# Down waves and gate steps in turn, gate weights half a chunk at a time, and a 26th buffer, in a mixture-of-experts layer

## The chip, the cores and the metric

The kernel runs on one core of a Trainium2 chip. The metric is the device time of one execution in microseconds (us). The core has a matrix engine (TensorE, shown as PE, its weight loads as PEld), a vector engine (VectorE, DVE), a scalar engine (ScalarE, ACT), a general engine (GpSimd, POOL) and a sequencer for transfers (SyncE, SP). 16 DMA engines move data between device memory (HBM) and the on-chip buffer (SBUF). Matmuls write to PSUM.

## The reference

One layer of a decoder on 256 tokens of width 2048, all in float32:

```
proj = rms_norm(x) @ w_in                       # 2048 x 4608: conv gates, q, k, v
h = x + [norm(conv(...)), norm(attention(...))] @ w_out     # 2048 x 2048
xt = rms_norm(h)
# top group of 4, then the top 2 of its 8 experts, for each token
h = h + sum over 2 experts of w * (silu(xt @ w_gate[e]) * (xt @ w_up[e])) @ w_down[e]
out = h + sigmoid(rms_norm(h) @ w_ple_gate) * (p @ w_ple)   # w_ple_gate 2048 x 2048
```

There are 32 experts, each with gate and up weights of 2048 x 512 and down weights of 512 x 2048, so every weight of every expert is read once: 403 MB of the 479 MB that the kernel reads.

## The kernel before, in words

**Buffers and transfers.** Nearly all data lives in a ring of `NSLOT` = 25 buffers of 8 KB per partition (1 MiB each). `want` (L63) lists every weight load in order. `pump` (L66) issues loads from that list, on SP's queue, as long as a buffer is free after what `reserve` holds back; `free` (L80) returns buffers and calls `pump`. So the order of the list and the places of the `free` calls in the program fix when each load can start. SP works in order: a load whose buffer is still being read holds up all later ones.

**Projections.** The input projection and the output projection (L332 to L823) split each float32 weight tile into a rounded part (`nc.scalar.copy`, L340) and a remainder (`tensor_sub`, L341), and multiply with three matmuls. The tiles of this stage leave the ring as it ends, and loads for the experts move in.

**Experts.** `select` and `gather` (L919, L938) pick up to 32 tokens for each of four experts, a *wave*, and transpose them into `xg`: eight waves. `gate_up` (L955) runs a wave's gate and up products; its rows are taken four at a time (`j4`), gate first, then up, and after each such group the four experts' buffers are freed. For the first row group of wave 0 the weights come in tiles that hold one row block of all four experts. There the gathers of wave 0 stand between the products:

```
                    if first and jj == 1:
                        gather(0, 4 if n == 0 else 12)
                if first and n == 0:
                    gather(0, 8)
```

After a wave's hidden values are transposed, `down_rows` (L1003) multiplies them with the down weights: waves 0 to 3 for all 2048 columns, waves 4 to 7 for the first 1024. `outputs` (L1051) scales a result into a rounded part `yh` (ScalarE) and a remainder `yl` (VectorE), and `scatter` (L1058) adds it to the tokens by matmul.

**The tail.** The output has four column chunks of 512 (`TC`, L149). Once a chunk of h is complete, `rows` (L1125) transposes it into `hs`, and eight *gate steps* (`gate_step`, L1149, twelve matmuls each) multiply it with 512 rows of `w_ple_gate`; `prep_pg` (L1114) splits those weights two steps ahead into three buffers. Chunks 0 and 1 are complete after `down_rows(7)`. For chunks 2 and 3 waves 4 to 7 run as `down_wave` (L1092), four loads each. Lines 1225 to 1247 set the order by hand: all eight gate steps of chunk 0, then chunk 2's four waves with chunk 1's steps, then chunk 3's four waves with chunk 2's steps. Then chunk 3's own eight steps and the output follow.

Of the kernel before, what the change touches and what calls it, by code (L numbers as in the profile page):

```python
# [21 lines left out]
CAP = 32  # L22
NW = NE // 4
NSLOT = 25
RING = 4096
NROW = 4
# [4 lines left out]
def kernel(ctx: ExitStack, tc: tile.TileContext, I, out):  # L31
# [74 lines left out]
    for i, (name, c0, hf) in enumerate(units):  # L106
        src = w_in_v[:, 8 * hf:8 * hf + 8, c0:c0 + 256]
        if i == 0:
            want((name, hf), [128, 2, 4, 256], [lambda: x_load(0), src[:, 0:4], lambda: x_load(1), src[:, 4:8]])
        else:  # L110
            want((name, hf), [128, 8, 256], src)
        if i == 1:
            want("x", None, [lambda: x_load(2), lambda: x_load(3)])
        if i == 3:
            want("small", None, [lambda: small_loads()])
    w_out_v = w_out.rearrange("(k p) n -> p k n", p=128)
    KORD = [2, 3, 0, 1]
# [4 lines left out]
    def want_gu(w):  # L122
        for j4 in range(4):
            for nm, wt in (("g", w_gate), ("u", w_up)):
                if w == 0 and j4 == 0:
                    for j in range(4):
                        want((nm, "0", j), [128, 4, 512],
                             wt[0:4].rearrange("e (p j) f -> p j e f", j=16)[:, j])
                    continue
                for e in range(4 * w, 4 * w + 4):  # L130
                    want((nm, e, j4), [128, 4, 512],
                         wt[e].rearrange("(p j) f -> p j f", j=16)[:, 4 * j4:4 * j4 + 4, :])
# [27 lines left out]
    for w in range(NW):  # L160
# [4 lines left out]
        if w == 5:  # L165
            want("p", [128, 2, 256], p.rearrange("(t p) k -> p t k", p=128))
            for k in range(2):
                want(("ple", k), [128, 2048], w_ple[128 * k:128 * k + 128, :])
    want_pg(0, 2, 3)
    want_pg(1)  # L170
    for ci in (2, 3):
        for w in range(NROW, NW):
            want_d(w, *TC[ci])
        want_pg(ci)

# [7 lines left out]
    cvs = alloc([128, 2048], F32, "cvs")  # L183
    et = C.tile([128, 5, 2, 32], F32, name="et")
    vec = et.rearrange("p a b c -> p (a b c)")[:, 0:128]
# [3 lines left out]
    def small_loads():  # L189
        for r, nm in ((88, "q_norm"), (89, "k_norm")):  # L190
            for h in range(2):
                nc.sync.dma_start(vec[r:r + 1, 64 * h:64 * h + 64], I[nm])
        nc.sync.dma_start(vec[48:72, :], I["conv_w"][0].rearrange("t (k p) -> (t k) p", p=128))
        for r0, nm, n in ((72, "out_norm_conv", 8), (80, "out_norm_attn", 8),
                          (16, "norm_ffn", 16), (32, "norm_ple", 16), (0, "norm_mix", 16)):
            nc.sync.dma_start(vec[r0:r0 + n, :], I[nm][0].rearrange("(k p) -> k p", p=128))

    pump()
# [20 lines left out]
    rb = lambda ap, n: bass.AP(tensor=ap.tensor, offset=ap.offset, ap=[[0, 128], [1, n]])  # L219
    sink = C.tile([128, NH], F32, name="sink")  # L220
    nc.gpsimd.dma_start(sink, rb(I["sinks"], NH))
# [8 lines left out]
    for s in range(2):  # L230
# [11 lines left out]
                            base=-1, channel_multiplier=-1)  # L242
    slope = C.tile([128, 2, NH], F32, name="slope")
    for h in range(NH):
# [6 lines left out]
    nc.gpsimd.dma_start(gffn, I["norm_ffn"][0].rearrange("(p j) -> p j", j=16))  # L251
    wr = C.tile([128, 16, 36], F32, name="wr")
    nc.gpsimd.dma_start(wr[:, :, 0:NG], I["w_group"][0].rearrange("(k p) n -> p k n", p=128))
    nc.gpsimd.dma_start(wr[:, :, NG:36], I["w_router"][0].rearrange("(k p) n -> p k n", p=128))
    nsink = C.tile([128, NH], F32, name="nsink")
    nc.gpsimd.tensor_scalar(nsink, sink, -1.0, None, op0=OP.mult)
# [50 lines left out]
    def vec_cols():  # L307
        pv = ps()
        nc.tensor.transpose(pv[:, 0:90], vec[0:90, :], ident[0:90, 0:90])
        nc.vector.tensor_copy(vT[:, 0:90], pv[:, 0:90])  # L310
        nc.vector.scalar_tensor_tensor(gqk, vT[:, 88:89], HD ** -0.5, vT[:, 89:90], op0=OP.mult, op1=OP.mult)
        nc.gpsimd.tensor_mul(wr, wr, g_ffn_k[:, :, None].to_broadcast([128, 16, 36]))

# [107 lines left out]

    rq = C.tile([128, 2, NH], F32, name="rq")
    prq = [None]
# [151 lines left out]
    def evac_in(name, pt):  # L575
# [263 lines left out]
    gm = rt[:, :, 6:7]  # L839
    E, key, ex, aw, rk = (et[:, i] for i in range(5))  # L840
    top = C.tile([128, 2, 2, 8], F32, name="top")
# [48 lines left out]

    cnt = C.tile([128, 32], F32, name="cnt")
    cnti = C.tile([1, 40], I32, name="cnti")
    ov = C.tile([128, 2, 32], F32, name="ov")

    def overflow_counts():
        pc = ps()
        for tt in range(2):
            nc.tensor.matmul(pc[:, 0:32], tri[:, 1], asg[:, tt], start=tt == 0, stop=tt == 1)
        nc.vector.tensor_scalar(cnt, pc[:, 0:32], float(CAP), 0.0, op0=OP.subtract, op1=OP.max)
        nc.vector.tensor_copy(cnti[0:1, 0:32], cnt[0:1, :])  # L900
        nc.vector.tensor_reduce(cnti[0:1, 32:33], cnti[0:1, 0:32], axis=AX.X, op=OP.max)
        nc.vector.tensor_scalar(ov, rk, float(CAP), None, op0=OP.is_gt)
        nc.vector.tensor_mul(ov, ov, aw)

# [50 lines left out]
    def gate_up(w):  # L955
        pt = pa()
        g = xg[w]
        for j4 in range(4):
            for n, nm in enumerate("gu"):
                for jj in range(4):  # L960
                    j = 4 * j4 + jj
                    for e in range(4):
                        first = w == 0 and j4 == 0
                        wt = arrived[nm, "0", jj][:, e, :] if first else arrived[nm, 4 * w + e, j4][:, jj, :]
                        nc.tensor.matmul(pt[32 * e:32 * e + 32, n, :], g[:, j, 32 * e:32 * e + 32],  # L965
                                         wt, start=j == 0, stop=j == 15, tile_position=(0, 32 * e))
                    if first:
                        if n == 1 and jj == 3:
                            reserve(1)
                        free()  # L970
                    if first and jj == 1:
                        gather(0, 4 if n == 0 else 12)
                if first and n == 0:
                    gather(0, 8)
                if not first:
# [27 lines left out]
    def down_rows(w):  # L1003
# [165 lines left out]
    def gate_product(ci):  # L1169
        kq = TC[ci][1] // 256  # L1170
        steps = pg_steps(ci)
        for i, (n, q) in enumerate(steps):
# [3 lines left out]
            gate_step(ci, i, pt, True)  # L1176
            prep_pg(ci, i + 2)
            ns = slice(512 * n, 512 * n + 512)
# [10 lines left out]
    gather(0, 0, 2)  # L1189
    gather(0, 2, 2)  # L1190
    weights()
# [27 lines left out]

    def steps(ci, n):  # L1220
        for _ in range(n):
            next(gates[ci])


    steps(0, 2)
    squares(0)
    rows(1)
    squares(1)
    steps(0, 6)
    po = pa()  # L1230
    for w, k in zip(range(NROW, NW), (1, 1, 1, 0)):
        steps(1, k)
        y = down_wave(w, *TC[2])
        steps(1, 1)
        scatter(po, w, y, w == NROW, w == NW - 1)
    add_down(po, *TC[2])
    steps(1, 1)
    rows(2)
    squares(2)
    po = pa()  # L1240
    for w, k in zip(range(NROW, NW), (2, 2, 2, 1)):
        steps(2, k)
        y = down_wave(w, *TC[3])
        if w == NW - 1:
            nc.scalar.activation(junk, eps, AF.Sqrt)
            steps(2, 1)
        scatter(po, w, y, w == NROW, w == NW - 1)
    early = [two(0), None, two(1), None]

# [8 lines left out]
    add_down(po, *TC[ci])  # L1258
    rows(ci)
    preload(1)  # L1260
    preload(2)
# [22 lines left out]
    def overflow():  # L1284
# [3 lines left out]
        ecur = C.tile([128, 1], F32, name="ecur")  # L1288
        ohe = C.tile([128, 32], F32, name="ohe")
        wc = C.tile([128, 2], F32, name="wc")  # L1290
# [120 lines left out]
```

## Time and profile before

| | |
|---|---|
| median of three runs | 1383.34 us (1383.12 to 1383.89) |
| profiled execution, its own time | 1383.49 us |
| its span, first to last instruction | 1381.7 us |
| PE busy | 1141.4 us (83%) |
| VectorE, ScalarE, POOL busy | 413.3, 265.5, 125.7 us |
| moved by DMA | 484.29 MB, mean 351 GB/s, 421 GB/s in the best slices |
| one wave's scaled output (L1054, L1055) | ScalarE 0.69 us, VectorE 0.75 us |
| one split of weights (L340, L341) | ScalarE 1.05 us, VectorE 1.2 to 1.4 us |

1.8 us of the profiled execution lie outside its span. "Granted clock" (PEclk) is the share of TensorE's full 2.4 GHz; the lower level is 1.2 GHz, and a figure between the two is a stretch with some of each. A wait is idle time of an engine, put down to the instruction or landing that ended it. Matmuls overlap in the pipe, so the distance between their starts, not their length, says how fast PE goes.

### The profile page before, as it was taken

How to read it: one execution, taken by the hardware profiler on the slowest of the kernel's cores; microseconds unless marked ns; L12 is line 12 of the kernel's file. 1: busy time of each engine (PE TensorE's matmuls, PEld its weight loads, DVE VectorE, ACT ScalarE, POOL GpSimd, SP SyncE). 2: the span in 40 equal slices, each digit the busy share in tenths (PEclk: the TensorE clock that was granted, in tenths of full speed). 3: DMA queues.
4: the chain of work that ended last, by engine and by line, in shares of the span. 5: the costliest groups of instructions: out<-in, count | busy, mean ns of one | idle time of the engine just before them, and what ended most of it. 6: DMA issues, size and time to landing. Idle time of an engine off the chain costs nothing.

```text
span 1381.7 us, 14910 instructions
## 1 busy us (share of the span) xinstructions
PE 1141.4 (83%) x6123; PEld 633.9 (46%) x6124; DVE 413.3 (30%) x625; ACT 265.5 (19%) x435; POOL 125.7 (9%) x152
## 2 busy tenths in 40 slices
PE   7999999999997786678668676877897865589997
PEld 6888777888762251215115121412431511146555
DVE  5747887555311100201110020110110120144435
ACT  5435555443101000000000000000010000033324
POOL 3215567000000000000000000000000000000000
PEclk9999999999999799889899989989898999989999
DMA  8982247876899999999999999999999999997991
GB/s 246 343 282 77 77 130 261 322 234 236 318 390 420 421 421 421 421 421 421 421 421 421 421 420 421 413 422 421 413 422 420 415 421 421 412 355 278 393 363 63
DMA packets 129141, 484.29 MB, mean 351 GB/s; under 512 B 7924, under 2 KB 45228, under 8 KB 88876
## 3 DMA queue, kind: packets, MB, share of 16 engines
q1 hardware_dynamic: 128076, 480.59, 88.4%
q0 software_dynamic: 992, 2.69, 0.6%
q8 instruction: 50, 0.82, 0.2%
q14 instruction: 23, 0.19, 0.0%
HBM read 478.80 MB, written 4.19 MB: 350 GB/s over the span
## 4 chain that ended last, share of the span: by engine, by line
DMA 54%; PE 33%; DVE 6%; ACT 4%; issue 1%; POOL 1%; SPq 1%; ACTq 0%; DVEq 0%
DMA ld<-in_w_up_dram 34%; DMA ld<-in_w_down_dram 17%; PE pat L762 5%; PE pst L943 4%; PE pat L965 3%; PE pat L763 2%; PE pst L1098 2%; PE pat L740 2%; PE pat L742 2%; PE pat L741 2%; DMA ld<-in_w_in_dram 2%; DVE wsp L341 1%; ACT wsp L340 1%; PE pst L1081 1%; PE pat L1159 1%
## 5 line engine op out<-in xcount | busy, mean ns | idle before, releaser
L965 PE MATMUL pat<-ld,xg 128*32 128x512 f32 x2048 | 333.4, 677 | 104.6 <-DMA ld<-in_w_up_dram 55.2
L965 PEld LDWEIGHTS pat<-ld,xg 128*32 128x32 f32 x2048 | 78.1, 121 | 348.2 <-issue 154.9
L762 PE MATMUL pat<-xs,wsp 128*128 128x512 f32 x544 | 197.1, 405 | 0.0
L1015 PE MATMUL pst<-ld,wv 128*32 128x512 f32 x768 | 146.2, 702 | 56.7 <-DMA ld<-in_w_down_dram 52.0
L341 DVE TENSOR_TENSOR wsp<-ld,wsp 128x1024 fp32r<-128x1024 f32 x91 | 131.3, 1447 | 82.0 <-ACT wsp L340 82.0
L763 PE MATMUL pat<-xs,wsp 128*128 128x256 f32 x544 | 153.4, 282 | 0.3 <-DVE wsp L341 0.3
L945 DVE TENSOR_TENSOR xg<-pst,gffn 128x512 f32<-128x512 f32 (+1 forms) x33 | 22.3, 675 | 404.2 <-PE pst L943 404.2
L340 ACT CAST wsp<-ld 128x1024 fp32r<-128x1024 f32 x104 | 108.0, 1048 | 90.7 <-PE pat L742 44.0
L943 PEld LDWEIGHTS pst<-sel,x 128*128 128x128 f32 x512 | 112.6, 311 | 9.2 <-PE pat L965 5.0
L762 PEld LDWEIGHTS pat<-xs,wsp 128*128 128x128 f32 x544 | 103.6, 190 | 28.2 <-issue 2.8
L943 PE MATMUL pst<-sel,x 128*128 128x128 f32 x512 | 114.7, 384 | 0.0
L1015 PEld LDWEIGHTS pst<-ld,wv 128*32 128x32 f32 x768 | 32.4, 124 | 164.7 <-DMA ld<-in_w_down_dram 101.0
L992 ACT ACTIVATE sg<-pat 128x512 f32<-128x512 f32 x8 | 4.8, 597 | 531.4 <-PE pat L965 531.4
L763 PEld LDWEIGHTS pat<-xs,wsp 128*128 128x128 f32 x544 | 104.0, 191 | 0.6 <-DVE wsp L341 0.6
L1055 DVE SCALAR_TENSOR_TENSOR yl<-pst,sw,yh 128x512 fp32r<-128x512 f32 x32 | 23.9, 746 | 224.5 <-ACT yh L1054 224.5
L1054 ACT ACTIVATE yh<-pst,sw 128x512 fp32r<-128x512 f32 x32 | 22.0, 688 | 237.7 <-PE pst L1015 180.8
L936 POOL TENSOR_TENSOR sel<-sel,et 128x128 f32<-128x128 f32 x16 | 6.1, 400 | 651.4 <-DVE sel L934 651.4
L1061 PE MATMUL pat<-yl,wv 128*128 128x512 f32 x64 | 32.7, 511 | 28.3 <-DVE yl L1055 28.3
L740 PE MATMUL pat<-wsp,mx 128*128 128x512 f32 (+1 forms) x128 | 49.8, 389 | 0.1
L742 PE MATMUL pat<-wsp,mx 128*128 128x512 f32 (+1 forms) x128 | 49.0, 383 | 0.0
L741 PE MATMUL pat<-wsp,mx 128*128 128x512 f32 (+1 forms) x128 | 49.0, 383 | 0.0
L341 DVE TENSOR_TENSOR wsq<-ld,wsq 128x1024 fp32r<-128x1024 f32 x32 | 38.6, 1222 | 33.6 <-ACT wsq L340 30.1
(275 smaller groups left out, 1076.4 us busy)
## 6 DMA issues: line engine op xcount, KB each, us to landing
ld<-in_w_gate_dram SPq DMA_DIRECT2D x128, 1024.0 KB, 19.8
ld<-in_w_up_dram SPq DMA_DIRECT2D x128, 1024.0 KB, 19.8
ld<-in_w_down_dram SPq DMA_DIRECT2D x128, 1024.0 KB, 19.7
ld<-in_w_in_dram SPq DMA_DIRECT2D x35, 1024.0 KB, 12.4
ld<-in_w_out_dram SPq DMA_DIRECT2D x16, 1024.0 KB, 12.5
ld<-in_w_ple_gate_dram SPq DMA_DIRECT2D x16, 1024.0 KB, 16.5
x<-in_x_dram SPq DMA_DIRECT2D x8, 256.0 KB, 6.8
spill<-x POOLq DMA_DIRECT2D x8, 256.0 KB, 5.6
```

What stands on the lines that cost most here:

```text
L340: copy(t[:, :, 0], src)
L341: eng.tensor_sub(t[:, :, 1], src, t[:, :, 0].bitcast(F32))
L740: nc.tensor.matmul(o, mh, ws[:, kk, 0, cs], start=first, stop=False)
L741: nc.tensor.matmul(o, mh, ws[:, kk, 1, cs], start=False, stop=False)
L742: nc.tensor.matmul(o, ml, ws[:, kk, 0, cs], start=False, stop=last)
L762: nc.tensor.matmul(pt[:, b, :], ws[:, kk, 0, bs], xk, start=first, stop=False)
L763: nc.tensor.matmul(pt[:, b, 0:256], ws[:, kk, 1, bs], xk[:, 0:256], start=False, stop=last)
L943: nc.tensor.matmul(pt[:, 128 * jj:128 * jj + 128], hmid[tt][:, j::16], sel[w][:, tt], start=tt == 0, stop=tt == 1)
L965: nc.tensor.matmul(pt[32 * e:32 * e + 32, n, :], g[:, j, 32 * e:32 * e + 32], wt, start=j == 0, stop=j == 15, tile_position=(0, 32 * e))
L1015: nc.tensor.matmul(pts[n][32 * e:32 * e + 32, :], hv[:, j, 32 * e:32 * e + 32], d[:, 512 * n:512 * n + 512], start=j == 0, stop=j == 3, ti ...
L1061: nc.tensor.matmul(po[:, tt], sT(w)[:, 128 * tt:128 * tt + 128], y[i], start=start and i == 0, stop=stop and i == 1)
L1098: nc.tensor.matmul(pt[32 * e:32 * e + 32, :], hv[:, j, 32 * e:32 * e + 32], arrived["d", 4 * w + e, c0][:, j, :], start=j == 0, stop=j == ...
```

## The change

The ring has 26 buffers; room for the last one comes from a smaller scratch for POOL's DMA descriptors (`RING`), and from small tiles that are dropped or placed in `cvs`. The router's weights are loaded on SP's queue behind the eighth weight load instead of POOL's. In wave 0 the loads alternate between gate and up, row by row, and the gathers stand just before the rows that use them. In the tail gate weights are listed half a chunk (two loads) behind each wave, and one list `todo` of all 24 gate steps is worked off around the waves: one step between a wave and its scatter, and one or two after it.

```diff
-NSLOT = 25
-RING = 4096
+NSLOT = 26
+RING = 1024
@@ loads
+        if i == 7:
+            want("wr", None, [lambda: wr_loads()])
@@ want_gu
-            for nm, wt in (("g", w_gate), ("u", w_up)):
-                if w == 0 and j4 == 0:
-                    for j in range(4):
+            if w == 0 and j4 == 0:
+                for j in range(4):
+                    for nm, wt in (("g", w_gate), ("u", w_up)):
                         want((nm, "0", j), [128, 4, 512],
                              wt[0:4].rearrange("e (p j) f -> p j e f", j=16)[:, j])
-                    continue
+                continue
@@ order of the loads in the tail
-    want_pg(0, 2, 3)
-    want_pg(1)
-    for ci in (2, 3):
-        for w in range(NROW, NW):
-            want_d(w, *TC[ci])
-        want_pg(ci)
+    order = [(2, w) for w in range(NROW, NW)] + [(3, w) for w in range(NROW, NW)]
+    halves_ = [(0, 1), (1, 0), (1, 1), (2, 0), None, (2, 1), None, (3, 0)]
+    for (ci, w), nxt_ in zip(order, halves_):
+        want_d(w, *TC[ci])
+        if nxt_:
+            want_pg(nxt_[0], 2 * nxt_[1], 2 * nxt_[1] + 1)
+    want_pg(3, 2, 3)
@@ router weights
+    def wr_loads():
+        for c0, n, nm in ((0, NG, "w_group"), (NG, NE, "w_router")):
+            nc.sync.dma_start(wr[:, :, c0:c0 + n], I[nm][0].rearrange("(k p) n -> p k n", p=128))
@@ vec_cols
-        nc.gpsimd.tensor_mul(wr, wr, g_ffn_k[:, :, None].to_broadcast([128, 16, 36]))
@@ evac_in
+            if u == 0:
+                nc.gpsimd.tensor_mul(wr, wr, g_ffn_k[:, :, None].to_broadcast([128, 16, 36]))
@@ gate_up
+            if w == 0 and j4 == 0:
+                for j in range(4):
+                    if j == 2:
+                        gather(0, 2, 2)
+                    for n, nm in enumerate("gu"):
+                        for e in range(4):
+                            block(j, n, e, arrived[nm, "0", j][:, e, :])
+                        if n == 1 and j == 3:
                             reserve(1)
                         free()
+            else:
+                if w == 0:
+                    gather(0, 4 * j4)
+                for n, nm in enumerate("gu"):
...
@@ down_rows, wave 7
+            y = outputs(pts[1], w)
             rows(0)
-            sums(1, outputs(pts[1], w))
+            sums(1, y)
@@ the tail
-    steps(0, 2)
     squares(0)
-    rows(1)
-    squares(1)
-    steps(0, 6)
+    steps(2)
     po = pa()
-    for w, k in zip(range(NROW, NW), (1, 1, 1, 0)):
-        steps(1, k)
+    for w in range(NROW, NW):
         y = down_wave(w, *TC[2])
-        steps(1, 1)
+        steps(1)
         scatter(po, w, y, w == NROW, w == NW - 1)
+        if w < NW - 1:
+            steps(1)
+            if w == NROW:
+                rows(1)
+                squares(1)
+            steps(1)
     add_down(po, *TC[2])
-    steps(1, 1)
+    steps(1)
     rows(2)
+    steps(1)
     squares(2)
+    steps(3)
     po = pa()
-    for w, k in zip(range(NROW, NW), (2, 2, 2, 1)):
-        steps(2, k)
+    for w in range(NROW, NW):
         y = down_wave(w, *TC[3])
         if w == NW - 1:
             nc.scalar.activation(junk, eps, AF.Sqrt)
-            steps(2, 1)
+        steps(1)
+        if w == NW - 1:
+            prep_pg(last, 0)
         scatter(po, w, y, w == NROW, w == NW - 1)
+        if w < NW - 1:
+            steps(1)
```

Also, the last chunk's second split stands behind `rows(3)`, and the weights of overflowing tokens (`ov`) are made only if a token overflows.

## Rows read from the trace of the kernel before

**Rows 1.** Stretches: length, busy time of each engine (instructions), granted clock, DMA share, GB/s.
```profile
352.90:389.20 36.30, 35.60 (x226) 23.11 (x227) 12.65 (x54) 4.30 (x12) 2.26 (x6) 1.00 0.87 331
389.20:1212.10 822.90, 614.16 (x3286) 234.15 (x3278) 93.63 (x175) 33.10 (x51) 4.55 (x12) 0.90 1.01 419
...
1226.00:1230.00 4.00, 4.00 (x11) 3.14 (x12) 2.42 (x3) 0.07 (x1) 0.00 (x0) 0.57 1.05 387
...
1235.00:1262.00 27.00, 25.54 (x127) 18.28 (x126) 12.02 (x13) 15.42 (x26) 0.00 (x0) 1.00 0.58 197
1262.00:1336.00 74.00, 69.18 (x391) 41.23 (x392) 32.00 (x39) 18.45 (x24) 0.00 (x0) 1.00 1.05 391
```
**Rows 2.** Waits of PE, 355 to 1382: total, times, longest.
```profile
PE pat L965 <- DMA ld<-in_w_up_dram: 55.2, 41, 1.5
```
**Rows 3.** Waits of SP's queue, 352 to 392.
```profile
SPq L76 <- PE pat L965: 31.4, 9, 11.2
```
**Rows 4.** Waits of PE, 1217 to 1340, all.
```profile
PE pat L1061 <- ACT yh L1054: 6.1, 4, 3.6
PE pat L1159 <- ACT hs L1140: 1.3, 1, 1.3
PE pat L1061 <- DVE yl L1055: 1.2, 4, 0.3
PE pat L1160 <- DVE wsq L341: 0.8, 1, 0.8
PE pat L1159 <- ACT wsq L340: 0.7, 1, 0.7
```
**Rows 5.** Timeline of PE, first wave: start, us, operation, count.
```profile
361.69 3.73 PE L943 MATMUL pst<-sel,x 128*128 128x128 f32 x16
365.36 1.92 PE L965 MATMUL pat<-ld,xg 128*32 128x512 f32 x16
```
**Rows 6.** Timeline of VectorE, first wave: copies of a half and a whole gather.
```profile
363.71 0.42 DVE L945 TENSOR_TENSOR xg<-pst,gffn 128x256 f32<-128x256 f32 x1 [1.97 <-PE pst L943]
...
371.00 0.69 DVE L945 TENSOR_TENSOR xg<-pst,gffn 128x512 f32<-128x512 f32 x1 [3.33 <-PE pst L943]
```
**Rows 7.** Timeline of PE, rest of the first wave.
```profile
384.20 13.94 PE L965 MATMUL pat<-ld,xg 128*32 128x512 f32 x128
398.07 14.24 PE L943 MATMUL pst<-sel,x 128*128 128x128 f32 x64
```
**Rows 8.** Timeline of PE, the tail.
```profile
1212.15 5.04 PE L1015 MATMUL pst<-ld,wv 128*32 128x512 f32 x25 [0.64 <-DMA ld<-in_w_down_dram]
...
1227.33 0.63 PE L1159 MATMUL pat<-wsq,hs 128*128 128x512 f32 x1
1227.75 0.63 PE L1160 MATMUL pat<-wsq,hs 128*128 128x512 f32 x1
...
1255.97 3.64 PE L1098 MATMUL pst<-ld,wv 128*32 128x512 f32 x32
...
1260.11 0.39 PE L1161 MATMUL pat<-wsq,hs 128*128 128x512 f32 x1
1260.34 0.40 PE L1159 MATMUL pat<-wsq,hs 128*128 128x512 f32 x1
...
1335.70 3.90 PE L1098 MATMUL pst<-ld,wv 128*32 128x512 f32 x32
```
**Rows 9.** DMA issues: engine, count, KB each, median us to landing.
```profile
ld<-in_w_in_dram SPq DMA_DIRECT2D x35, 1024.0 KB, 12.4
...
wr<-in_w_router_dram POOLq DMA_DIRECT2D x1, 256.0 KB, 7.7
...
wr<-in_w_group_dram POOLq DMA_DIRECT2D x1, 32.0 KB, 9.8
```
**Rows 10.** Timeline of SP and of ScalarE: the load behind the eighth, its first split.
```profile
33.31 3.10 SPq L76 DMA_DIRECT2D ld<-in_w_in_dram  x1
...
53.86 1.05 ACT L340 CAST wsp<-ld 128x1024 fp32r<-128x1024 f32 x1 [1.07 <-PE pat L762]
```

More of the change, by code (lines that the diff above doesn't have):

```diff
@@ L123, in want_gu @@
         for j4 in range(4):
-            for nm, wt in (("g", w_gate), ("u", w_up)):
-                if w == 0 and j4 == 0:
-                    for j in range(4):
+            if w == 0 and j4 == 0:
+                for j in range(4):
+                    for nm, wt in (("g", w_gate), ("u", w_up)):
                         want((nm, "0", j), [128, 4, 512],
                              wt[0:4].rearrange("e (p j) f -> p j e f", j=16)[:, j])
-                    continue
+                continue
+            for nm, wt in (("g", w_gate), ("u", w_up)):
                 for e in range(4 * w, 4 * w + 4):
@@ L183 @@
     cvs = alloc([128, 2048], F32, "cvs")
-    et = C.tile([128, 5, 2, 32], F32, name="et")
+    et = C.tile([128, 4, 2, 32], F32, name="et")
     vec = et.rearrange("p a b c -> p (a b c)")[:, 0:128]
@@ L196, in small_loads @@
             nc.sync.dma_start(vec[r0:r0 + n, :], I[nm][0].rearrange("(k p) -> k p", p=128))
+    wr = C.tile([128, 16, 36], F32, name="wr")
+    def wr_loads():
+        for c0, n, nm in ((0, NG, "w_group"), (NG, NE, "w_router")):
+            nc.sync.dma_start(wr[:, :, c0:c0 + n], I[nm][0].rearrange("(k p) n -> p k n", p=128))
     pump()
@@ L219 @@
     rb = lambda ap, n: bass.AP(tensor=ap.tensor, offset=ap.offset, ap=[[0, 128], [1, n]])
-    sink = C.tile([128, NH], F32, name="sink")
+    sink, nsink = cvs[:, 1924:1940], cvs[:, 1940:1956]
     nc.gpsimd.dma_start(sink, rb(I["sinks"], NH))
@@ L242 @@
                             base=-1, channel_multiplier=-1)
-    slope = C.tile([128, 2, NH], F32, name="slope")
+    slope = cvs[:, 1956:1988].rearrange("p (a h) -> p a h", a=2)
     for h in range(NH):
@@ L251 @@
     nc.gpsimd.dma_start(gffn, I["norm_ffn"][0].rearrange("(p j) -> p j", j=16))
[L252 to L255, printed above, removed]
     nc.gpsimd.tensor_scalar(nsink, sink, -1.0, None, op0=OP.mult)
@@ L420, in k_norm @@
         nc.scalar.copy(r2b, pt[:, 0:256])
-    rq = C.tile([128, 2, NH], F32, name="rq")
+    rq = cvs[:, 1988:2020].rearrange("p (a h) -> p a h", a=2)
     prq = [None]
@@ L839 @@
     gm = rt[:, :, 6:7]
-    E, key, ex, aw, rk = (et[:, i] for i in range(5))
+    E, key, aw, rk = (et[:, i] for i in range(4))
+    ex = key
     top = C.tile([128, 2, 2, 8], F32, name="top")
@@ L888, in weights @@
         nc.vector.tensor_mul(aw, aw, w1.to_broadcast([128, 2, 32]))
-    cnt = C.tile([128, 32], F32, name="cnt")
     cnti = C.tile([1, 40], I32, name="cnti")
-    ov = C.tile([128, 2, 32], F32, name="ov")
     def overflow_counts():
@@ L898, in overflow_counts @@
             nc.tensor.matmul(pc[:, 0:32], tri[:, 1], asg[:, tt], start=tt == 0, stop=tt == 1)
+        cnt = w2([128, 32], "cnt")
         nc.vector.tensor_scalar(cnt, pc[:, 0:32], float(CAP), 0.0, op0=OP.subtract, op1=OP.max)
@@ L901, in overflow_counts @@
         nc.vector.tensor_reduce(cnti[0:1, 32:33], cnti[0:1, 0:32], axis=AX.X, op=OP.max)
-        nc.vector.tensor_scalar(ov, rk, float(CAP), None, op0=OP.is_gt)
-        nc.vector.tensor_mul(ov, ov, aw)
     xg, sel = {}, {}
@@ L957, in gate_up, with block @@
         g = xg[w]
+        def block(j, n, e, wt):
+            nc.tensor.matmul(pt[32 * e:32 * e + 32, n, :], g[:, j, 32 * e:32 * e + 32],
+                             wt, start=j == 0, stop=j == 15, tile_position=(0, 32 * e))
         for j4 in range(4):
[L959 to L968, printed above, removed]
+            if w == 0 and j4 == 0:
[6 more added lines that the diff above has]
+                        if n == 1 and j == 3:
                             reserve(1)
                         free()
[L971 to L975, printed above, removed]
+            else:
+                if w == 0:
+                    gather(0, 4 * j4)
+                for n, nm in enumerate("gu"):
+                    for jj in range(4):
+                        for e in range(4):
+                            block(4 * j4 + jj, n, e, arrived[nm, 4 * w + e, j4][:, jj, :])
                     if j4 == 1 and n == 1 and w + 1 < NW:
@@ L1176, in gate_product @@
             gate_step(ci, i, pt, True)
-            prep_pg(ci, i + 2)
+            if (ci, i + 2) < (last - 1, len(steps)):
+                prep_pg(ci, i + 2)
             ns = slice(512 * n, 512 * n + 512)
@@ L1189 @@
     gather(0, 0, 2)
-    gather(0, 2, 2)
     weights()
@@ L1218, with steps @@
     gates = [gate_product(ci) for ci in range(last)]
-    def steps(ci, n):
+    todo = [next_ for ci in range(last) for next_ in [gates[ci]] * len(pg_steps(ci))]
+    def steps(n):
         for _ in range(n):
-            next(gates[ci])
-    steps(0, 2)
+            next(todo.pop(0))
     squares(0)
-    rows(1)
-    squares(1)
-    steps(0, 6)
+    steps(2)
     po = pa()
-    for w, k in zip(range(NROW, NW), (1, 1, 1, 0)):
-        steps(1, k)
+    for w in range(NROW, NW):
         y = down_wave(w, *TC[2])
-        steps(1, 1)
+        steps(1)
         scatter(po, w, y, w == NROW, w == NW - 1)
+        if w < NW - 1:
[4 more added lines that the diff above has]
+            steps(1)
     add_down(po, *TC[2])
-    steps(1, 1)
+    steps(1)
     rows(2)
+    steps(1)
     squares(2)
+    steps(3)
     po = pa()
-    for w, k in zip(range(NROW, NW), (2, 2, 2, 1)):
-        steps(2, k)
+    for w in range(NROW, NW):
         y = down_wave(w, *TC[3])
@@ L1245 @@
             nc.scalar.activation(junk, eps, AF.Sqrt)
-            steps(2, 1)
+        steps(1)
+        if w == NW - 1:
+            prep_pg(last, 0)
         scatter(po, w, y, w == NROW, w == NW - 1)
+        if w < NW - 1:
+            steps(1)
+    assert not todo
     early = [two(0), None, two(1), None]
@@ L1259 @@
     rows(ci)
+    prep_pg(ci, 1)
     preload(1)
@@ L1288, in overflow @@
         ecur = C.tile([128, 1], F32, name="ecur")
-        ohe = C.tile([128, 32], F32, name="ohe")
+        ovt = ring([128, 3, 32], "ovt")
+        ohe, ov = ovt[:, 2], ovt[:, 0:2]
+        nc.vector.tensor_scalar(ov, rk, float(CAP), None, op0=OP.is_gt)
+        nc.vector.tensor_mul(ov, ov, aw)
         wc = C.tile([128, 2], F32, name="wc")
```

## Prediction

> **What bounds the kernel now.** I read the page's 40 slices first, then busy time and transfer rate by stretch, then who waited for whom on PE and on SP, and last the timelines of the two places that the change edits.
>
> By stretch [rows 1] the kernel has three regimes. From 389.2 to 1212.1 us the DMA engines move 419 GB/s and are busy for the whole time (share 1.01); PE waits for weights there (the largest item is 55.2 us for the up weights [rows 2]). This stretch is bound by bytes: it ends earlier only if more has been loaded when it begins. Just before, from 352.9 to 389.2, PE is busy for 35.6 of 36.3 us and the DMA manages 331 GB/s; SP sits on its next load for 31.4 us until a matmul of the first gate/up wave frees a buffer [rows 3]. The ring is full, PE empties it too slowly, and DMA time that the next 820 us need is lost. After 1212.1 it turns again: the rate drops to 197 GB/s from 1235 to 1262 and is 391 after, but PE waits for no transfer at all. From 1217 to 1340 it waits only for other engines' results, 10.1 us in all [rows 4]. So the tail is bound by PE plus these waits, with a hole of 27 × (1 − 197/391) = 13.4 us in the DMA stream that PE does not notice.
>
> **First wave and 26th buffer.** PE work stays the same: gather matmuls at 3.73 us per eight, gate/up matmuls at about 0.93 us per block of four experts [rows 5] (a float32 matmul leaves two records); only the order changes. Before, the first eight blocks alternate with four gathers of 3.7 us, so eight loads' buffers come free over 22 us, some 373 GB/s. After, eight blocks follow two half gathers. New are five waits of PE for VectorE's copy of a gather that is used at once: 0.42 us for a half and 0.69 for a whole one [rows 6], about 0.2 more for the last matmul to drain, so 2 × 0.65 + 3 × 0.95 = 4.1 us. PE stands in order, so everything behind them moves too, the frees included. PE's sum from 361.7: 2 × (1.87 + 0.65 + 3.7) for the first row group, 0.4 for the transposes, 2 × (3.73 + 0.95 + 6.97) for the next two (6.97 is half of 13.94 for 64 matmuls [rows 7]): 397.8. There 24 buffers are free again, as before at 398.07, but eight of them by about 374 instead of 384, and sixteen by 386 instead of 391.
>
> What the DMA gains: a load is 1.049 MB, 2.49 us at the page's 421 GB/s. Idle from 352.9 to 389.2 is 36.3 × (1 − 331/421) = 7.7 us. After, about 1 us remains near 365, where the first frees come, and about 1.5 near 420: by the buffer count 23 + 24 − 2 = 45 loads can be issued before the next wave's gathers (14.24 us [rows 7]); the next free is at 397.8 + 14.6 + 3.7 + 0.95 + 3.5 = 420.6, and at full rate the 45th load lands at about 423 (an estimate: 22 loads of 2.49 after a 23rd at 368), so only one or two are in flight for a moment. Recovered: 7.7 − 2.5 = 5.2 us. The 26th buffer puts one more load ahead of the byte-bound stretch: 2.5 us. PE reaches the down rows some 3 us later than before, but catches up in the second wave, where it waited for DMA anyway. Together **7.7 us**; low end 2.5 (the extra buffer alone), high end 10.2 (no idle left).
>
> **The tail.** Work is again equal: 24 gate steps of 12 matmuls at a pitch of 0.23 us (2.75 us a step), eight waves of 3.6 us, eight scatters [rows 8]. Order and waits change:
> - Row group 0: the wave's second output is scaled before rows(0) instead of behind its copies on ScalarE and VectorE. Of 3.56 + 0.30 us of waiting [rows 4] about 0.5 stays. The first gate step now waits instead for rows(0)'s halves, queued behind that scaling on VectorE: it starts near 1224.4 instead of 1227.3 and meets one more wait of 0.7. Net 2.2.
> - Waits for splits (0.7 + 0.8): gone, since two steps no longer follow at once on the next chunk's rows; 1.5. They come back if a wave's output and a gate-weight split meet on ScalarE.
> - Chunk 2 of rows: four gate steps now lie between its transposes and its first use; the 1.3 us for hs goes.
> - Last three scatters of chunk 3: a gate step of 2.75 us now stands between a wave and its scatter, and covers ScalarE's and VectorE's 1.5 us. 1.1 us each, 3.4.
> Sum **8.4 us**; last wave at 1335.7 − 8.4 = 1327.3 on the old time axis.
>
> Does the DMA allow that? With the new list the last wave needs 42 loads after the ones that landed at 1212.15 [rows 8]. At 391 GB/s one takes 2.68 us: 1212.15 + 112.6 = 1324.8, if the stream never pauses. Each group frees four down loads and two gate-weight units per 12.9 us of PE (three steps, a wave, a scatter of about 1) where DMA needs 16.1, and 13 buffers are ahead, so it should not pause; the hole of 13.4 us closes. The two limits are 2.5 us apart, PE the later. Low end 2 us (waits come back as waits for loads), high end 11. Gate-weight splits are queued on ScalarE ahead of a wave's output; by the two lists this concerns one load only that is listed behind that wave (chunk 2's second half behind wave 5), and the step between wave and scatter covers its 2.7 us. From the last wave to the end the same instructions follow (one split moved behind rows); 0.
>
> **The rest.** The router weights go from POOL's queue to SP's, behind the eighth weight load; they took 9.8 and 7.7 us to land [rows 9], and they cost SP at least about 1.2 us each, as POOL, and at most those 17.5. The next load was issued at 33.31, so with the median of 12.4 us it landed near 45.7; its first split at 53.86 waited for PE, not for it [rows 9, 10]: 8.2 us of cover, growing afterwards. I take 0; at the upper bound 9.3 us of PE in a stretch where PE is the limit, less what k and v's loads gain from the cleared start. The Trainium skill (DMA: Bandwidth & Descriptors, Specifications) gives 512 B as the least transfer for line rate; runs of 16 and 128 B stand here in front of weights, so its rule speaks against the move, and by it the sum would lose part of that upper bound. No row shows these runs on SP's queue. Their product with the norm moves on POOL to just ahead of the first q square, whose sums give way twice before PE reads it: 0. Smaller scratch for POOL's descriptors: the two kvt copies and the eight spill stores could wait for room, but what stood ahead of them with the most runs, the router weights, is gone from that queue, and nothing in this run reads the spill: 0. Fewer small tiles, aliases in cvs, overflow weights made only on overflow (two small VectorE operations beside a DMA-bound wave): 0.
>
> **Sum.** 1383.49 (the profiled execution, 1.8 outside its span, 0.15 over the median of 1383.34) − 7.7 − 8.4 = **1367.4 us**.
>
> **Rivals.**
> 1. *Wave 0 fills the ring again* (chance 0.14). PE's five new waits and the next wave's gathers stop the frees while the DMA is ahead; only the extra buffer stays: 1383.5 − 2.5 − 8.4 = 1372.6. For it: the gathers' 14.24 us without a free. Against: 45 loads are issued before.
> 2. *The tail swaps its waits* (0.14). DMA and PE limits lie 2.5 us apart, so small disorder turns waits for outputs into waits for loads: gain 2, 1383.5 − 7.7 − 2 = 1373.8.
> 3. *Both limits are met in full* (0.16): 10.2 + 11 gone, 1362.3.
> 4. *Router loads starve the projection* (0.04): 9.3 us lost of the forecast, 1376.7.
> 5. *Slower: TensorE's clock* (0.05). If the tail becomes DMA-bound, PE idles before each wave. After PE's waits before 1226 the matmul pitch was 0.42 us at 1227 and 0.23 at 1260 [rows 8]: the granted clock from 1226 to 1230 was 0.57 of full [rows 1], that is mostly the 1.2 GHz level. At the lower level a gate step costs 2.4 us more; seven of the 24 steps eat the whole forecast, and twelve would give 1383.5 − 16.1 + 28.8 = 1396. Against: from 1235 to 1336 the clock is 1.00 through waits of up to 1.3 us [rows 1, 4]. The Trainium skill (TensorE: Matmul & The Clock Gate, What's actually happening) says of this that "the default state is throttled, and activity releases the throttle"; the rows at 1227 agree.
>
> **How the numbers follow.** The forecast has 0.47. Its own range is 1363 to 1372; 8 in 10 need rivals 1 to 3 too: 1360 to 1376. A change of 0.2% (2.8 us) is about what a measurement of this kernel can tell from none. Slower: 0.03, from rival 5 beyond eight steps; within 0.2%: 0.03, rivals 5 and 2 together; faster: 0.94.
>
> **What would show it.** SP's wait for first-wave matmuls falls well under 31.4 us, the rate from 365 to 415 is near 420, and the up weights that PE meets first as a wait arrive some 8 us earlier; the last half-row load of wave 7 lands near 1204.5 instead of 1212.1. In the tail no hole of 197 GB/s, PE's waits for yh, yl and hs under 3 us, a few waits of under 1 us for down loads, the last wave about 16 us earlier and the same 46 us behind it. I am wrong if PE waits for loads of several us stand between 1205 and 1325, if the clock there falls under 0.9, or if the projection ends later than at 361.7.

## The result, and the profile after

The changed kernel takes **1363.16 us** (median of four runs, 1362.52 to 1363.85), the kernel before 1383.38 (four runs beside it): ratio 0.9853, 95% interval 0.9836 to 0.9871, 20.2 us less. The forecast was 1367.4, in a range of 1360 to 1376: the sign and the places are right, the gain is 4.1 us larger than the 16.1 of the forecast. The profiled execution took 1363.11, its span is 1361.3 us; all accounting below goes from span to span, 20.4 us.

The stretches of the changed kernel, in the columns of [rows 1]:

```profile
352.90:389.20 36.30, 33.00 (x221) 18.96 (x223) 11.66 (x53) 3.27 (x11) 2.05 (x5) 1.00 0.94 384
389.20:1200.00 810.80, 611.69 (x3280) 238.02 (x3268) 94.02 (x174) 33.20 (x51) 4.55 (x12) 0.88 1.01 420
...
1200.00:1210.00 10.00, 8.05 (x30) 1.97 (x31) 0.75 (x1) 0.69 (x1) 0.00 (x0) 0.66 1.04 391
...
1235.00:1262.00 27.00, 27.00 (x152) 17.34 (x154) 12.35 (x13) 12.40 (x18) 0.00 (x0) 1.00 1.04 393
1262.00:1320.00 58.00, 58.00 (x333) 37.48 (x326) 27.50 (x34) 17.03 (x23) 0.00 (x0) 1.00 1.03 389
```

Against [rows 1]: the stretch ahead of the byte-bound one rises from 331 to 384 GB/s, the byte-bound one is as fast as it was, and the hole of 197 GB/s is gone. From 1235 to 1320 PE is shown busy for the whole time and the DMA engines too (share 1.03 to 1.04).

The first wave, timeline of PE (start, us, operation, count, idle time before and what ended it), beside [rows 5, 7]:

```profile
360.18 1.99 PE L949 MATMUL pst<-sel,x 128*128 128x128 f32 x8
362.68 3.64 PE L965 MATMUL pat<-ld,xg 128*32 128x512 f32 x32 [0.52 <-DVE xg L951]
366.25 2.02 PE L949 MATMUL pst<-sel,x 128*128 128x128 f32 x8
368.78 3.64 PE L965 MATMUL pat<-ld,xg 128*32 128x512 f32 x32 [0.51 <-DVE xg L951]
```

Half a gather, a wait for its copy, two row blocks, twice: the order that was forecast, but begun 1.5 us earlier than [rows 5]. SP's wait for this wave, beside [rows 3]:

```profile
SPq L76 <- PE pat L965: 25.5, 9, 10.1
```

The tail. First all waits of PE from 1190 to 1361, beside [rows 4]; then the timeline of PE, and four rows of that of its weight loads (PEld):

```profile
PE pst L1025 <- DMA ld<-in_w_down_dram: 6.6, 6, 1.5
PE pst L1145 <- DVE x L1117: 0.7, 1, 0.7
PE pat L1072 <- DVE yl L1066: 0.3, 1, 0.3
PE pat L1170 <- ACT hs L1151: 0.3, 1, 0.3
```

```profile
1202.99 6.53 PE L1025 MATMUL pst<-ld,wv 128*32 128x512 f32 x26 [1.51 <-DMA ld<-in_w_down_dram]
...
1215.38 0.50 PE L1170 MATMUL pat<-wsq,hs 128*128 128x512 f32 x1 [0.28 <-ACT hs L1151]
...
1314.71 4.24 PE L1109 MATMUL pst<-ld,wv 128*32 128x512 f32 x32
```
```profile
1216.11 0.19 PEld L1172 LDWEIGHTS pat<-wsq,hs 128*128 128x128 f32 x1 [0.43 <-DVE hs L1152]
...
1217.36 0.19 PEld L1170 LDWEIGHTS pat<-wsq,hs 128*128 128x128 f32 x1 [0.49 <-ACT hs L1151]
...
1218.09 0.19 PEld L1172 LDWEIGHTS pat<-wsq,hs 128*128 128x128 f32 x1 [0.43 <-DVE hs L1152]
...
1315.33 2.28 PEld L1109 LDWEIGHTS pst<-ld,wv 128*32 128x32 f32 x25 [0.47 <-DMA ld<-in_w_down_dram]
```

All of the 6.6 us for down loads lie at or before 1203, in the last row wave. Of the 10.1 us of [rows 4], 0.3 for yl and 0.3 for hs are left. The last half-row load is met at 1202.99 instead of 1212.15, the first gate step starts at 1215.38 instead of 1227.33, the last wave at 1314.71 instead of 1335.70 [rows 8]. The rows of the weight loads count below, for PE's idle time does not show them: the first gate step stood three times for halves of `hs`, and the last wave 0.5 us for the fourth and last of its loads (six records, that is three matmuls with one load each, had gone before).

Where the time went, each as a difference of such starts. The forecast's net 2.2 for row group 0 stands in two lines, as it was worked out: the first gate step 2.9 us earlier (1224.4 instead of 1227.3), and one more wait of 0.7 behind its start.

| stretch | forecast | measured |
|---|---|---|
| projection, to the first gather | 0 | -1.51 |
| first gather to the last half-row load | -7.7 | -7.65 |
| from there to the first gate step | -2.9 | -2.79 |
| first gate step to the last wave | -5.5 | -9.04 |
| last wave to the end | 0 | +0.59 |
| sum | -16.1 | -20.40 |

### The profile page after: what moved, and what is told of

The parts are those of the page before. It is cut to its first block, busy times and chain, and to the rows that moved or that the text cites. A ratio compares the mean times of both kernels' runs of the same rounds, so it can differ in the third digit from the quotient of the medians.

```text
span 1361.3 us, 14898 instructions
## 1 busy us (share of the span) xinstructions
PE 1136.3 (83%) x6123; PEld 634.3 (47%) x6124; DVE 411.8 (30%) x623; ACT 266.3 (20%) x435; POOL 122.4 (9%) x150
## 4 chain that ended last, share of the span: by engine, by line
DMA 49%; PE 39%; DVE 5%; ACT 3%; SPq 2%; issue 1%; POOL 1%; DVEq 0%; ACTq 0%
DMA ld<-in_w_up_dram 35%; DMA ld<-in_w_down_dram 13%; PE pat L770 6%; PE pst L949 5%; PE pat L965 4%; PE pat L771 3%; PE pst L1109 2%; PE pat L748 2%; PE pat L750 2%; PE pat L749 2%; SPq L76 1%; ACT wsp L346 1%; PE pst L1092 1%; PE pat L1170 1%; PE pat L1171 1%
## 5 line engine op out<-in xcount | busy, mean ns | idle before, releaser
L965 PE MATMUL pat<-ld,xg 128*32 128x512 f32 x2048 | 325.6, 669 | 104.4 <-DMA ld<-in_w_up_dram 55.3
L1025 PE MATMUL pst<-ld,wv 128*32 128x512 f32 x768 | 152.2, 755 | 52.1 <-DMA ld<-in_w_down_dram 47.1
```

The source lines that it names most:

```text
L1025: nc.tensor.matmul(pts[n][32 * e:32 * e + 32, :], hv[:, j, 32 * e:32 * e + 32], d[:, 512 * n:512 * n + 512], start=j == 0, stop=j == 3, ti ...
```

## The experiments

Twelve kernels ran. "More" and "less" are against the changed kernel's 1363.16; ratios are against the kernel before, which ran beside each, and go by the means. The intervals of 25 buffers, of the scatters at once and of rows(0) first overlap that of the changed kernel, so there the times alone do not show a difference, and the traces have to carry the claim.

**25 buffers, and the first wave of before.** The first takes back `NSLOT`, the second the order of wave 0's loads and gathers, each alone; a third takes back both.

```diff
-NSLOT = 26
+NSLOT = 25
```
```diff
@@ gate_up, wave 0 (and its loads: four g, then four u)
-                    if j == 2:
-                        gather(0, 2, 2)
...
+                    if first and jj == 1:
+                        gather(0, 4 if n == 0 else 12)
```

> The changed kernel with 25 buffers again, all else kept. Theory (a buffer is one load more ahead of the byte-bound stretch, 1.049 MB at 421 GB/s): 2.5 us more than the changed kernel, 1365.7 us, with the last half-row load of wave 7 landing 2.5 us later and the tail as long as it was. Rival (the new order of wave 0 keeps the DMA busy by itself, the buffer adds nothing): 1363.2. Second rival (the tail needs the 13th load ahead): 1367 or more, the extra time lying behind wave 7.

> The changed kernel with the old order of wave 0: its loads gate rows first, its gathers between the products. Theory (frees come later, DMA idles 5.2 us more before the byte-bound stretch): 1368.4 us, and the rate from 360 to 390 near 310 GB/s. Rival (the gain of the front comes from the extra buffer and the earlier end of the projection, PE's new waits eat the rest): 1363 to 1364, or less, since the five waits of PE for gathers are gone.

> The changed kernel with the first wave of before and 25 buffers; the tail and the router loads stay changed. Theory (the two front terms add: one is an idle DMA in 353 to 389 us, the other one more load ahead of the byte-bound stretch): 2.3 + 4.6 = 6.9 us more than the changed kernel, 1370.1, or 1370.9 by the forecast's 7.7. Rival (a full ring hides a better first wave, and a better first wave needs no 26th buffer, so each alone gives most of it): no more than 1368.5.

Measured: 25 buffers 1365.50 (ratio 0.9876, 0.9860 to 0.9893), 2.3 more; the old wave 0 1367.74 (0.9889, 0.9873 to 0.9906), 4.6 more; both 1371.06 (0.9911, 0.9897 to 0.9925), 7.9 more. The old wave 0 alone brings the idle DMA back (windows):

```profile
352.90:389.20 36.30, 35.59 (x227) 22.62 (x229) 12.65 (x54) 4.04 (x12) 2.05 (x5) 1.00 0.85 324
```

The terms were 2.5, 5.2 and 7.7. The traces say the same without the tail: from the first gather to the start behind the last half-row load the three take 845.59, 848.04 and 850.35 us, the changed kernel 842.81 and the kernel before 850.46; that is 2.8, 5.2 and 7.5. The terms add within what the runs can tell: the one does not replace the other, and rival 1 (the ring fills again) falls.

**The old tail; its list alone; its order alone.** The first kernel has the old list of loads, the old order of the steps and rows(0) ahead of the second output; the second only the list, the third only the order.

```diff
@@ list (second kernel)
-    halves_ = [(0, 1), (1, 0), (1, 1), (2, 0), None, (2, 1), None, (3, 0)]
...
+    want_pg(0, 2, 3)
+    want_pg(1)
...
@@ order (third kernel): the loops of before, with
+    for w, k in zip(range(NROW, NW), (1, 1, 1, 0)):
...
```

> The changed kernel with the whole old tail: list of loads, order of gate steps, rows(0) before the second output. Theory (the tail gave 11.2 us by what the two traces show, beside the front's 9.2): 1374.4 us. Rival (front and tail overlap: an earlier start of the tail only meets a DMA that lags): 1368 to 1372.

> The changed kernel, with only the order of the loads in the tail put back (each gate chunk's weights as a block behind the down weights); the order of the work stays the new one. Theory (the list is needed): wave 4 of chunk 2 now stands behind three gate steps but its four loads come behind the two blocks of gate weights again, so DMA, which is at its rate until about 1230 us, brings them when PE has been waiting; PE waits for down loads or gate weights 4 to 8 us in all between 1215 and 1320, and the time is 1367 to 1371. Rival (the list is a matter of tidiness, 20 buffers ahead cover any order): no wait over 1 us behind 1205, 1363.2 within 1.5.

> The changed kernel, with only the order of PE's work in the tail put back (gate steps two at a time before and after the waves, no step between wave and scatter except where it was); the list of loads stays the new one, and the second output stays ahead of rows(0). Theory (the waits that went were waits for ScalarE and VectorE, so the order of the work is what counts): the waits for hs, wsq and the three scatters return, 1.3 + 1.5 + 3 x 1.64 = 7.7 us: 1370.9, or more if loads now arrive behind their use. Rival (the gain came from the even stream of loads): the time stays at 1363.2 within 1.5.

Measured: old tail 1371.33 (0.9925, 0.9906 to 0.9944), 8.2 more; old list alone 1371.66 (0.9913, 0.9896 to 0.9929), 8.5 more; old order alone 1371.03 (0.9906, 0.9889 to 0.9923), 7.9 more. (One of the old tail's four runs took 1374.87, the others 1370.99 to 1371.47, so its ratio lies further off than its median.) So the two halves do not add. Either one taken back costs as much as both: the new order without the new list gains nothing, nor the list without the order. They lose it in different ways. With the old order PE waits for the other engines again (waits of PE, 1190 to 1361):

```profile
PE pat L1072 <- ACT yh L1065: 2.7, 3, 0.9
PE pat L1170 <- ACT hs L1151: 1.6, 2, 1.3
PE pat L1072 <- DVE yl L1066: 1.1, 4, 0.3
...
PE pat L1171 <- DVE wsq L347: 0.8, 1, 0.8
PE pat L1170 <- ACT wsq L346: 0.7, 1, 0.7
```

With the old list the first wave of chunk 2 stands too early for its loads (timeline of PE, then the window around it):

```profile
1221.28 1.02 PE L1108 MATMUL pst<-ld,wv 128*32 128x512 f32 x2 [0.43 <-DMA ld<-in_w_down_dram]
1223.90 1.05 PE L1108 MATMUL pst<-ld,wv 128*32 128x512 f32 x2 [1.61 <-DMA ld<-in_w_down_dram]
1226.60 1.56 PE L1108 MATMUL pst<-ld,wv 128*32 128x512 f32 x2 [1.64 <-DMA ld<-in_w_down_dram]
1229.27 5.86 PE L1108 MATMUL pst<-ld,wv 128*32 128x512 f32 x26 [1.12 <-DMA ld<-in_w_down_dram]
```
```profile
1228.00:1232.00 4.00, 2.88 (x17) 0.76 (x20) 0.00 (x0) 0.00 (x0) 0.00 (x0) 0.50 1.05 388
```

The loads come 2.7 us apart, one transfer each, and the wave lasts 13.8 us instead of 3.6. Idle time shows 4.8 us of it; the rest is matmuls between the landings and, behind the last landing, 26 records at half clock, 1.2 GHz (granted 0.50 from 1228 to 1232; they take 5.86 us, at full clock 3.62). Rival 2 (waits for outputs become waits for loads) is thus a real mechanism, which the new list keeps away.

**Two single waits of the tail.** The scatter of chunk 3's first three waves at once behind its wave, and rows(0) ahead of the second output.

```diff
@@ chunk 3, first three waves
-        steps(1)
...
         scatter(po, w, y, w == NROW, w == NW - 1)
...
-            steps(1)
+            steps(2)
```
```diff
@@ down_rows(7)
-            y = outputs(pts[1], w)
             rows(0)
-            sums(1, y)
+            sums(1, outputs(pts[1], w))
```

> The changed kernel; in chunk 3 alone the gate step between a wave and its scatter stands behind the scatter (two steps there), for the first three waves. By the starts of PE's instructions (a scatter that waits takes 1.64 us longer from start to start) this costs 3 x 1.64 = 4.9 us: 1368.1. By the idle time that the waits show (1.1 us each, as the forecast had it) 3.4 us: 1366.6. Rival (the wait is hidden by something else, for the two steps behind make up for it): 1363.2 within 1.

> The changed kernel, with rows(0) ahead of the second output of the last row wave again, nothing else. Theory (PE's wait for yh behind rows(0) was on the path): the wait for yh of about 3.5 us returns and the first gate step stands 2.2 to 2.8 us later, at 1217.6 to 1218.2: 1365.4 to 1366.0. Rival (the first gate step needs the halves that rows(0) makes, so it waits either way, and the sums are then late where rows(0) was): the first gate step within 0.7 us of 1215.4, 1363.2 within 1.

Measured: the scatters 1366.41 (0.9878, 0.9859 to 0.9897), 3.3 more. Each wait is back (timeline of PE, one of three):

```profile
1283.97 3.64 PE L1109 MATMUL pst<-ld,wv 128*32 128x512 f32 x32
1288.49 0.49 PE L1072 MATMUL pat<-yh,wv 128*128 128x512 f32 x1 [0.89 <-ACT yh L1065]
1289.28 0.50 PE L1072 MATMUL pat<-yl,wv 128*128 128x512 f32 x1 [0.29 <-DVE yl L1066]
...
1295.64 3.64 PE L1109 MATMUL pst<-ld,wv 128*32 128x512 f32 x32
```

Wave to wave it is 11.67 and 11.70 us where the changed kernel has 10.20: 1.5 each, between the 1.1 and the 1.64 of the two countings, for two steps that follow each other take 0.15 us less than with a wave or a scatter between. The third costs only 0.9 (11.60 instead of 10.68), because the changed kernel's third wave itself stood for its fourth load. Together 3.9 us on PE; the last wave then no longer stands for its load (0.6), and 3.3 are left, which is what the times show. So the count by idle time (3.4) meets the time only because the smaller stand for the load made up for what it left out.

rows(0) first: 1364.80 (0.9862, 0.9846 to 0.9879), 1.6 more; the profiled one of its four took 1366.76, the others 1364.57 to 1364.97. Its timeline and window:

```profile
1217.42 0.80 PE L1071 MATMUL pat<-yh,wv 128*128 128x512 f32 x1 [3.56 <-ACT yh L1064]
...
1219.67 0.63 PE L1169 MATMUL pat<-wsq,hs 128*128 128x512 f32 x1
```
```profile
1217.00:1222.00 5.00, 4.57 (x10) 3.29 (x11) 3.26 (x5) 2.53 (x6) 0.00 (x0) 0.50 1.04 388
```

The wait of [rows 4] is back at its old length, and behind it the clock is at its lower level for 5 us: matmuls start 0.43 us apart, as in [rows 8] at 1227. The first gate step, the last row shown, starts 4.3 us later than in the changed kernel (0.4 of it lies ahead of this place), where 2.2 to 2.8 were expected, and takes 4.23 us, where it takes 3.75 there. So in this execution the wait costs twice, once as idle time and once in the matmuls behind it. By how much the second varies from run to run no trace here shows.

**The router weights' queue.** Done alone on the kernel before, and undone on the changed kernel with 25 buffers.

```diff
@@ kernel before: only this
+            want("wr", None, [lambda: wr_loads()])
...
-    nc.gpsimd.dma_start(wr[:, :, 0:NG], ...
...
```

> The kernel before with one change: the router weights are loaded on SP's queue behind the eighth weight load, and multiplied on POOL at the first q. Theory (the projection ends 1.5 us earlier in the changed kernel because of this move, and all later stages follow): 1381.9 us, the first gather at 360.2. Rival (the 1.5 us come from elsewhere, and the short runs hold up the weights): 1383.4 or more.

> The changed kernel with the router weights' two loads on POOL's queue again, their product in its old place, and what that queue needs: 4096 for its scratch and 25 buffers. So it stands beside the 25-buffer kernel (1365.5, first gather at 359.4). Theory (the cleared start is what ends the projection 1.5 us earlier): first gather at 361.2 to 361.7, 1367.0. Rival (the projection's end moves by 1 us from one execution to the next, and the loads' queue is no cause): first gather within 0.7 of 360.2, 1365.5 within 0.7.

Measured: alone 1381.91 (0.9994, 0.9985 to 1.0004), which cannot be told from no change, and its first gather stands at 361.50 (before 361.69). Undone: 1366.71 (0.9881, 0.9865 to 0.9897) beside 1365.50 (0.9876, 0.9860 to 0.9893) with 25 buffers, and the first gather at 360.79, which is where the rival had it, while the time is near the theory's. In the eleven kernels that have the changed projection whole it stands at 359.4 to 361.2. The moved loads hold SP for 2.95 and 6.04 us (timeline of SP):

```profile
31.29 2.95 SPq L207 DMA_DIRECT2D wr<-in_w_group_dram  x1
34.28 6.04 SPq L207 DMA_DIRECT2D wr<-in_w_router_dram  x1
40.37 6.38 SPq L76 DMA_DIRECT2D ld<-in_w_in_dram  x4
```

The next weight load goes out at 40.37 instead of 33.31 [rows 10], and the projection ends no later for it: the cover held. Whether the 1.5 us of the projection come from this move, from the other edits to that stage or from the spread between executions stays open.

**Two attempts to go on.** Each gather of wave 0 in two parts, so that a copy runs beside the next part; and, on top of that, an unused matmul ahead of each group that waits for a load in the last row wave.

```diff
-                        gather(0, 2, 2)
+                        gather(0, 2, 1)
+                        gather(0, 3, 1)
-                    gather(0, 4 * j4)
+                    gather(0, 4 * j4, 3)
+                    gather(0, 4 * j4 + 3, 1)
@@ second kernel, down_rows(7)
+                        keep_warm(1)
```

> The changed kernel; each gather of the first wave in two parts (1 + 1 and 3 + 1 rows), so that VectorE's copy of the first part runs beside the gather of the second. PE's five waits for xg in the first wave (0.51 to 0.78 each, 3.1 us) fall under 1.2 us in all. Theory (the first frees come 0.5 us earlier and the ring is empty there, 295 GB/s from 360 to 370 us): 0.5 to 1.2 us less, 1362.0 to 1362.7. Rival (the stretch behind is bound by bytes, so only the first 0.5 us can count): 1363.2 within 0.4.

> The kernel with the split copies, and in the last row wave one extra matmul that nobody reads (identity by 512 columns) ahead of each of the eight matmul groups that wait for a load. Theory (PE idles 1.5 us before each load there, and the clock falls to 0.66 from 1200 to 1210; with work in the gap it stays up): granted clock of 0.9 or more from 1200 to 1210, the first gate step 1.1 us earlier than without, 1.1 us less than the kernel with the split copies alone. Rival (DMA's limit is met in the tail, so an earlier gate step only turns into a later wait): same within 0.4. Other rival: the extra matmuls push the ones behind them, up to 0.9 us more.

Measured: 1362.78 (0.9854, 0.9837 to 0.9870) and 1362.21 (0.9847, 0.9832 to 0.9863). Both intervals overlap that of the changed kernel; neither is shown to be faster. Yet both did what they should. The five waits are gone, 360 to 370 us rises from 295 to 311 and 310 GB/s, and with the extra matmuls the clock stays up:

```profile
1200.00:1210.00 10.00, 9.55 (x59) 3.33 (x57) 2.46 (x4) 1.37 (x2) 0.00 (x0) 1.00 1.04 392
```

The 26 records that took 6.53 us in the changed kernel take 3.62, and the first gate step starts at 1211.64, 3.7 us earlier. Then most of the gain is lost again in one place, the last wave of chunk 2, which takes 6.5 us instead of 3.6 (timeline of PE):

```profile
1257.85 1.32 PE L1120 MATMUL pst<-ld,wv 128*32 128x512 f32 x6
1260.83 3.62 PE L1120 MATMUL pst<-ld,wv 128*32 128x512 f32 x26 [1.66 <-DMA ld<-in_w_down_dram]
```

The last wave of chunk 3 starts at 1313.74, only 1.0 us earlier than in the changed kernel. In this kernel the tail cannot run ahead of its loads.

## Why the prediction was right, and where its sizes were off

**Front: right in size.** 7.65 us of 7.7, and by undoing 2.3 and 4.6 for its parts by the times, 2.8 and 5.2 by the traces (2.5 and 5.2). From the hundredth expert load on, loads are issued 9.2 us earlier than before (541.71 instead of 550.89), 7.7 beside the 1.5 of the projection. The five new waits of PE are 3.4 us (forecast 4.1). SP's wait fell from 31.4 to 25.5 us, less than "well under" said, for the gathers still stand there. The forecast left 2.5 us idle near 365 and 420; the first is there (295 GB/s from 360 to 370: 10 x (1 - 295/421) = 3.0 us), the second is not: 370 to 415 runs at 421.

**Tail: the right waits went, the term for them was too small.** The tail's term is 8.4, and 2.79 + 9.04 - 0.59 = 11.2 came. The part that was too small is "first gate step to the last wave": 5.5 forecast, 9.04 measured. By the starts of the same pieces of work before and after, it is made up so:

| seven waves, their scatters and what stood between | two transposes of rows | 23 gate steps | sum |
|---|---|---|---|
| forecast 3.4 | 1.3 | 1.5 - 0.7 | 5.5 |
| measured 37.03 - 32.08 = 4.95 | 3.16 - 1.58 = 1.58 | 68.18 - 65.67 = 2.51 | 9.04 |

Two causes:
- Idle time understates a wait of PE. Matmuls at full clock start 0.23 us apart and are shown 0.39 long, so a wait begins 0.16 late; and the first matmuls behind one start further apart (0.33 us). So three scatters gave 4.9 us and not 3.4. Among the gate steps, the two that waited for splits were 1.9 us too long before and not 1.5, and the one behind chunk 2's transposes took 3.74 us and takes 2.82, for a second wait that the idle time does not show; the other steps are 0.3 us longer in their new places.
- The forecast saw the clock at 0.57 from 1226 to 1230 [rows 1] and used it only against the change. It stands behind the wait for yh, so it goes with that wait: five matmuls 0.43 instead of 0.23 us apart, 1.0 us. The first gate step is hardly shorter for it (3.75 us instead of 3.80), because the one more wait that the forecast put at 0.7 did come, as the three short ones of the weight loads shown above. The gain of the clock, which the forecast left out, paid for it.

The stretch ahead of the first gate step came out at 2.79 of 2.9 partly by luck. The last row wave ran at a lower clock after (6.53 us for the 26 records behind that load, 5.47 before), a loss of 1.1 us inside the 2.79 which the forecast did not have; without it the stretch would have gained 3.9.

**The two limits: right, and closer than stated.** The DMA limit was put at 42 loads of 2.68 us behind the last half-row load: from 1202.99 that is 1315.6, and the last wave, begun at 1314.71, stood until 1315.33 for the last of these loads. The wave lost 0.6 us by it (4.17 us to the gate step behind it, other waves 3.57). Against the kernel before, which took 3.83 there, that is 0.34 of the "+0.59" behind the last wave; the other 0.25 lies after 1329.4, in chunk 3's own gate steps and the output, and its cause is open. PE and DMA now end together, so rival 3 is the nearest of the rivals (1362.3). The attempts show what follows: 3.7 us won on PE ahead of the tail became 1.0 at the last wave.

**Rival 5, slower by the clock,** did not occur: the clock is 1.00 from 1215 to 1320. It was under the 0.9 of "I am wrong if" only in the last row wave (0.61 from 1205 to 1210), which was so before as well (0.50 from 1210 to 1215). The old list with the new order does meet the rival's condition for one wave, at 0.50; of its 8.5 us the clock makes some 2.2 (5.86 instead of 3.62), the rest is the wait for the loads. The Trainium skill's rule (TensorE: Matmul & The Clock Gate, What's actually happening), that activity releases the throttle, agrees with the kernel with extra matmuls: 1.00 from 1200 to 1210 where the changed kernel has 0.66.

**Projection: sized 0, measured 1.5.** "Less what k and v's loads gain from the cleared start" named a gain without a size; no experiment shows that it is the cause. By the Trainium skill (DMA: Bandwidth & Descriptors, Specifications) runs under 512 B miss the line rate; here they held SP for 9.0 us and cost the kernel nothing that can be measured.

**What the single parts leave.** Undoing the front (7.9) and the tail (8.2), and doing the router move alone (1.2 below the kernel before), make 17.3 of 20.2 us. Some of the rest is the clock: the old tail on the changed front happened to run the end of its last row wave at full clock (3.62 us for the 26 records) and reached its first gate step at 1215.73 although the wait for yh was back. From its last half-row load to there it took 12.88 us, the kernel before 15.18, so this undoing understates the tail by up to 2.3 us.

## What to carry to other kernels

Order of work and order of loads are one change: take each back alone before crediting either, since here each alone was worth nothing and both together 8 us. Price a wait of PE from start to start, on the weight loads' rows too, and with the clock behind it, not by the idle time alone. Work out the limit of each engine for the stretch; where two limits meet within a microsecond, as here, the next gain has to come from both.

## What was not expected of the hardware

- The same 26 matmul records behind the last half-row load took 3.62, 5.47 or 6.53 us: with the extra matmuls (granted clock 1.00 from 1200 to 1210), before (0.50 from 1210 to 1215) and in the changed kernel (0.66 from 1200 to 1210). With one extra matmul of 1.1 us in each of PE's waits the clock held at 1.00 from 1183 to 1210, where the changed kernel has 0.75 and the kernel before 0.86. The place where it falls varies, though: the old tail on the changed front had 3.62 us without extra matmuls, at 0.81 over the same stretch.
- The rate of DMA in the tail goes with the size of the packets in which a load moves. The trace lists each packet: in the changed kernel one of 8 KB (gate and up weights) takes 314 ns on a DMA engine, one of 4 KB (half rows, gate weights of the output) 163, one of 2 KB (a wave's down weights for one chunk) 88, so 26.1, 25.1 and 23.2 GB/s for an engine. The two lists show it in the same stretch, the changed kernel first, then the old tail on the changed front, whose last half-row load is met at 1202.85:

```profile
1200.00:1205.00 5.00, 3.05 (x14) 0.73 (x18) 0.00 (x0) 0.00 (x0) 0.00 (x0) 0.71 1.04 389
```
```profile
1200.00:1205.00 5.00, 3.20 (x22) 0.81 (x26) 0.00 (x0) 0.21 (x1) 0.00 (x0) 1.00 1.03 410
```

  The first moves 810 packets of 2 KB and 70 of 4 KB there, the second only 4 KB ones; its rate falls to 403 and 388 from 1210 and 1215 on, when the 2 KB packets come. This rate sets the tail's limit now. An estimate from these rates: the 32 chunk loads at 409 GB/s instead of 387 would take some 4.7 us less; no run here tries it. (Before, the rate was 389 from 1215 to 1220 with 4 KB packets alone, 172 ns each; that dip has no known cause.)
